# A hybrid attention and mLSTM block: the list scheduler prices TensorE's change between 512- and 128-column matmuls, and the order of all instructions is drawn anew

## The chip, the cores and the metric

The kernel runs on one core of a Trainium2 chip. A core has TensorE (PE in the profile, its weight loads PEld), VectorE (DVE), ScalarE (ACT), GpSimd (POOL) and SyncE (SP), each of which works through its own queue in order; they meet through semaphores. The metric is the device time of one execution in microseconds, as a median of runs.

## What is computed

Two layers of a decoder block on 512 tokens of width 1024, in float32. Each layer normalises its input and projects it to twelve pieces, runs two branches and adds them up behind gates:

```python
h = rmsnorm(x, norm_g)
proj = h @ w_in
aq, ak, av, az, bqk, bv, bi, bf, bo, bz, ga, gb = jnp.split(proj, idx, axis=-1)
...
oa = diff_attention(q, k, v, lam)                   # q, k: RMS-normed and rotated heads of aq, ak
oa = rmsnorm(oa, attn_norm_g) * (1.0 - lam_init)
ya = (oa * jax.nn.silu(az)) @ w_out_a
...
hb = mlstm_chunkwise(mq, mk, mv, i_pre, f_pre)      # from silu(conv(bqk)), bv, bi, bf
hb = jax.nn.sigmoid(bo) * rmsnorm(hb, mlstm_norm_g) * jax.nn.silu(bz)
yb = hb @ w_out_b
u = jax.nn.sigmoid(ga) * ya + jax.nn.sigmoid(gb) * yb
return x + u @ w_o
```

`diff_attention` takes softmax over 512 causal keys for two maps of each of eight heads, subtracts the second times `lam`, and multiplies with the values. `mlstm_chunkwise` has eight heads too; the kernel computes it as one masked 512x512 product.

## The kernel before

Precision comes from splitting: a float32 operand is stored as a high part (`wh`, `hh`, `uh`, `sdh`), cut by ScalarE, and a low part (`wl`, `hl`, `ul`, `sdl`), the difference, made by VectorE, and each product is three matmuls (high·high, low·high, high·low; `mm3`). So every block of weights of 128x1024 that SyncE fetches (`wr`) costs ScalarE one CAST of 1024 columns and VectorE one subtraction of 1024 before TensorE can use it.

Most matmuls stream 512 columns into an accumulator of one PSUM bank (pool `ps_acc`, four buffers; the names are those of the projections: qk, av, az, bqk, bv, bo, bz, ga, gb, woa, wob, wo). Between them stand the branches:

- attention, for head h and query block j: `sc` (scores, 128·(j+1) columns; one PSUM buffer), then mask, maximum, exponential and normalisation on VectorE and ScalarE into `p`, then `ut` (TensorE transposes `p` in 128x128 blocks; one PSUM buffer shared with all transposes and norm sums), split into `uh` and `ul`, then `av` (512, 384, 256 and 128 columns), then `msp_a` (a matmul with ones that sums squares across partitions) and the gated output `oa`
- mLSTM, for head h: `dd` (decay, fetched from DRAM rows and exponentiated), `ms` and `ms2` (scores of 512, 384, 256 and 128 columns), `sdh` and `sdl` (their split), `num` (512 to 128 columns), `fo_d` and `den` (the row sum, a matmul of 512 columns with ones), then `msp_b` and `ob`
- transposes of 128 columns: `ht` (the normalised input), `qkt` (rotated q and k, `rot`), `ut`, and in each layer four of `gft`, `glf` and `gct` for the gates.

A sum of squares can be folded (`fold`, `ms_front`): ScalarE squares both halves of the partitions, VectorE adds them, and high and low part share one tile of 128 partitions, so that one matmul of 512 columns does what otherwise takes two (`hi_lo`). `TUNE["foldA"]` and `TUNE["foldM"]` name the heads that fold.

The program records all operations with their dependences (`Recorder.add`), and `Recorder.schedule` then draws the order of every engine at once. It is a list scheduler with a model of time: it takes the engine that can begin first and, among the instructions of that engine whose operands the model calls ready (`rt`), the one with the lowest key. An instruction's key is its due time, propagated back from its consumers with latencies and margins, plus `TUNE["bias"]` for its kind of tile. On top come penalties that depend on the moment: `drain` if ScalarE or VectorE changes its partition offsets, `late` if the operand has been ready for less than `risk` nanoseconds, `wdiff` if the instruction isn't ready yet. An operand that another engine makes for TensorE counts as ready `pemargin` nanoseconds after it is done and the modelled latency is over. The matmul's cost in the model is its columns over 2.4 plus 13.4 ns, at least 107.5. `TUNE["order"]`, `attn`, `ml` and the other numbers set in which order the pieces of the projections are recorded and between which of them the branches' steps fall.

All recorded instructions carry line 441 in the profile (449 with the change), the line of the recorder that issues them, so tiles tell them apart and lines don't. The four-product `seven` scheme at the end (`wo`) is the same on both sides.

Of the kernel before, what the change touches and what calls it, by code (L numbers as in the profile page):

```python
# [18 lines left out]
P = 128  # L19
# [16 lines left out]

TUNE = {
    "order": (
# [4 lines left out]
    ),  # L43
    "qkt": 5,
    "gct": 15,
    "gls": 6,
    "glf": 5,
    "attn": (1, 5, 5, 8, 9, 13, 15, 16, 19, 24),
    "a0": 23,
    "ap": 18,  # L50
    "a4": 7,
    "ml": (1, 9, 11, 12, 13, 28),
    "ahead": 3,
    "lc": 7,
    "slack": 4956.0,
    "margin": 72.0,
    "pemargin": 206.2,
    "wait": 333.1,
    "swpen": 141896579.9,
    "smargin": 51.6,  # L60
    "pwait": 0.7,
    "wdiff": 3673.3,
    "wsp": 4,
    "kact": (0, 2),
    "qsq": (1, 3),
    "foldA": (2, 3, 5),
    "foldM": (0, 1, 2, 3, 4, 7),
    "foldD": (0, 1, 2, 3, 4, 5, 6, 7),
    "warm": 18,
    "start": 'x0 ct ng w0 x1 w1 x2 x3',  # L70
    "prods": 'P1 P5 P2 P6 P3 P7 P4',
    "acl": 14,
    "gateA": 9,
    "gateM": 4,
    "actp": (0, 2, 3),
    "m0": 217,
    "mp": 15,
    "m4": 9,
    "slots": 20,
    "bias": {'av': 30400.0, 'msp_a': -4350.0, 'wl': 2200.0, 'wo': -3700.0, 'woh': -4650.0, 'ht': 29250.0, 'taz': -4050.0, 'ga': 25150.0, 'gt': -8800.0, 'p': -900.0, 'wo1_P': 27550.0, 'out_0_dram': -5850.0, 'p5_wo': -4950.0, 'rot': 12400.0, 'dq': -4400.0, 'oa': 450.0, 'dd': 31000.0, 'num': 20100.0, 'ld': -7300.0, 'ws1_wo': -2200.0, 'gw': -1100.0, 'hl': -600.0, 'sc': -1500.0, 'uz': -3750.0, 'mk': 7950.0, 'sbz': 4200.0, 'az': 12900.0, 'posi': 3200.0, 'msl_d': 1650.0, 's1_wo': 5000.0, 'msh_d': 6450.0, 'sq': -1400.0, 'warm': 3150.0, 'bo': -450.0, 'sdl': 150.0, 'ml': 16100.0, 'fo_b': 12850.0, 'ws0_wo': -900.0, 'wt1_wo': 1400.0, 'pb': 8800.0, 'sbo': 5350.0, 'qkt': 3900.0, 'junk': 7400.0, 'ulZ': 6400.0, 'bv': 650.0, 'bqk': -1750.0, 'uh': -3950.0, 'ms_b': -1100.0, 'ob': -400.0, 'uy': 1500.0, 'ms': 11100.0, 'ms_a': 1750.0, 'ones': 4150.0, 'msh_b': 8300.0, 'x1d': -3000.0, 'saz': 1000.0, 'xr': -3950.0, 'wo0_P': 450.0, 'qk1_0x': 2050.0, 'msh_a': 6050.0, 'rnh': -3150.0, 'gft': 6600.0, 'gct': 3100.0, 'kl': -700.0, 'qk1_2x': -800.0, 'gf': 1550.0, 'qk0_0x': -1600.0, 'qy': 7250.0, 'msl_a': 1400.0, 'x': -4550.0, 'eps': -600.0, 'wt0_wo': -2500.0, 'xn': 400.0, 'msl_b': 2150.0, 'rn': -400.0, 'glf': -3500.0, 'ss': 7600.0, 'sinv': 6150.0, 'ulA': -2650.0, 'epsc': -3000.0, 'ulB': 950.0, 'ulY': -300.0, 'tbz': 350.0, 'hh': 3700.0, 'fo_a': 6500.0, 'mx': -1800.0, 'gc': -150.0, 'mq': -1050.0, 'ang': 3150.0, 'qt': -2500.0, 'uhZ': -1250.0, 'em': -6800.0, 'ct': 1000.0, 'fo_d': 3850.0, 'par': -250.0, 'ks': 250.0, 'den': -400.0, 'sdh': -1000.0, 'cv': -300.0, 'ng': 3750.0, 'uhB': 300.0, 'rows': -300.0, 'zw': 50.0, 'qs': 1350.0, 'ctab': 950.0, 'gcol': 3400.0, 'ul': 1000.0, 'fb_b': 400.0, 'sums': 400.0, 'cosv': 250.0},  # L80
    "drain": 467.1,
    "risk": 268.4,
    "late": 912.7,
}


# [16 lines left out]
class Recorder:  # L103
# [61 lines left out]
    def add(self, eng, e, fn, a, k):  # L165
        i = len(self.ops)
        outs = [a[0]] + ([k["accum_out"]] if k.get("accum_out") is not None else [])
        ins = [x for x in list(a[1:]) + [v for n, v in k.items() if n != "accum_out"] if isinstance(x, bass.AP)]
        if fn == "matmul" and not k["start"] or k.get("accum_op") is not None:
            ins.append(a[0])  # L170
        preds = {}
        for kind, aps in (("r", ins), ("w", outs)):
            for ap in aps:
                name, quad, mask = self.region(ap)
                ws, rs = self.acc.setdefault(name, ([], []))
                if kind == "r" and ap.space == PSUM:

                    for j, q, m in rs:
                        if self.ops[j]["eng"] != eng:
                            preds.setdefault(j, 0)  # L180
                if kind == "w":
                    for j, q, m in rs:
                        if q & quad and m & mask and j != i:
                            preds.setdefault(j, 0)
                    rs[:] = [x for x in rs if x[0] != i and (x[1] & ~quad or x[2] & ~mask)]
                for j, q, m in ws:

                    whole = kind == "r" and ap.space == PSUM and any((m >> b) & 0xFFFF and (mask >> b) & 0xFFFF for b in (0, 16))
                    if (whole or q & quad and m & mask) and j != i:
                        preds[j] = 1  # L190
                if kind == "w":
                    ws[:] = [x for x in ws if x[0] != i and (x[1] & ~quad or x[2] & ~mask)]
                    ws.append((i, quad, mask))
                else:
                    rs.append((i, quad, mask))
                t = self.tiles.get(name)
                if t is not None and (not t["ops"] or t["ops"][-1] != i):
                    t["ops"].append(i)
        if eng == "PE":

            name, _, mask = self.region(a[0])
            for b in range(2):
                if mask >> (16 * b) & 0xFFFF:
                    j = self.bank.get((name, b))
                    if j is not None:
                        preds.setdefault(j, 0)
                    self.bank[name, b] = i
        cost = self.cost(eng, fn, a, k)
        if eng == "PE":
            self.pe_time += cost  # L210
        rows = None
        if eng in ("ACT", "DVE"):

            rows = tuple(x.offset // math.prod(list(x.tensor.shape)[1:]) for x in [a[0]] + ins[:1])
        self.ops.append({"eng": eng, "e": e, "fn": fn, "a": a, "k": k, "pre": preds, "cost": cost, "nom": self.pe_time, "rows": rows, "kind": a[0].tensor.name.rstrip("_0123456789")})

    @staticmethod
    def cost(eng, fn, a, k):
# [53 lines left out]
    def schedule(self):  # L272
        ops = self.ops
# [31 lines left out]
        for i in reversed(range(n)):  # L305
            o = ops[i]
# [12 lines left out]
        table = 6  # L319
        order = []  # L320
        at_rows = {"ACT": (0, 0), "DVE": (0, 0)}

        def admit(i):

# [13 lines left out]
        while len(order) < n:  # L338
# [5 lines left out]
            for e in engs:  # L344
                c = cand[e]
                if c is None:
                    c = []
# [9 lines left out]
            s, e = best  # L357
            pick = None
            for q, i in cand[e]:
                if q <= s + (TUNE["wait"] if e != "PE" else TUNE["pwait"]):  # L360
                    k = key[i] if e != "SP" else i
                    if e in at_rows and ops[i]["rows"] != at_rows[e]:
                        k += TUNE["drain"]
                    if s - q < TUNE["risk"] and e != "SP":
                        k += TUNE["late"]
                    if e == "ACT":
                        sets = self.ACT_SET.get(self.func(ops[i]))
                        if sets and table not in sets:
                            k += TUNE["swpen"]
                    if q > s:  # L370
                        k += TUNE["wdiff"]
                    if pick is None or k < pick[0]:
                        pick = (k, i, q)
            i = pick[1]
# [4 lines left out]
            o = ops[i]  # L379
            c = o["cost"]  # L380
            if e in at_rows:
                if o["rows"] != at_rows[e]:
                    s = max(s, free[e] + 115.0)
                at_rows[e] = o["rows"]
            if e == "ACT":
                sets = self.ACT_SET.get(self.func(o))
                if sets and table not in sets:
                    s = max(s, free[e] + 1283.0)
                    table = sets[0]
                    load = table  # L390
# [1255 lines left out]
```

## Time and profile before

| | |
|---|---|
| median of 3 runs | 1333.95 us (1333.81 to 1335.08) |
| span of the profiled execution, first to last instruction | 1333.4 us |
| TensorE busy | 1326.1 us, 6200 matmuls |
| VectorE busy | 1018.1 us |
| ScalarE busy | 907.4 us, 66 table loads |
| DMA | 148.15 MB, 111 GB/s on average |

The profile has no time of its own for the profiled execution besides its span, so 0.55 us of the median lie around a span. A row of the timeline gives the start of an instruction in us from the start of the span, its duration, engine, line, operation, output and inputs (buffer numbers left out), and in square brackets how long the engine had been idle and what ended that. Matmuls overlap each other: one of 512 columns is shown with some 0.39 us while the next begins 0.23 us after it. What a matmul costs is therefore read from starts, not from durations.

### The profile page before, as it was taken

What the parts mean: (1) busy time and instruction counts of PE and PEld (TensorE: products, weight loads), DVE (VectorE), ACT (ScalarE), POOL (GpSimd) and SP (SyncE); (2) the same over time, 40 slices, a digit from 0 to 9 for tenths busy, and PEclk for the clock granted to TensorE, in tenths of its full rate; (3) what the DMA queues carried; (4) which work ended last, traced back from release to release, by engine and by line L of the source; (5) the groups of instructions that cost most, each with busy time, mean ns of one, the idle gap of its engine ahead of it and who ended that gap; (6) DMA issues with size and microseconds to landing.
All of it is one profiled execution on the core that took longest, in us unless ns stands there. A gap on an engine that the chain in (4) does not pass through costs nothing.

```text
span 1333.4 us, 17564 instructions
## 1 busy us (share of the span) xinstructions
PE 1326.1 (99%) x6200; PEld 1096.4 (82%) x6200; DVE 1018.1 (76%) x1846; ACT 907.4 (68%) x1836; POOL 37.0 (3%) x44
## 2 busy tenths in 40 slices
PE   8999999999999999999999999999999999999998
PEld 7888888888888888888888888888888888888887
DVE  7898899786259967755888988997852698687466
ACT  5878888877237958743667787888762478687243
POOL 1000000000000000000200000000000000000000
PEclk9999999999999999999999999999999999999999
DMA  5222222323344433544832121223232444345546
GB/s 188 87 65 79 80 80 64 95 79 94 100 121 124 119 114 109 154 148 123 258 125 88 49 96 54 89 67 92 82 110 81 123 134 124 98 129 148 170 123 181
DMA packets 51274, 148.15 MB, mean 111 GB/s; under 512 B 6097, under 2 KB 12881, under 8 KB 51185
## 3 DMA queue, kind: packets, MB, share of 16 engines
q1 hardware_dynamic: 48880, 138.63, 33.5%
q0 software_dynamic: 2304, 8.39, 3.5%
q8 instruction: 49, 0.80, 0.3%
q14 instruction: 41, 0.33, 0.1%
HBM read 142.74 MB, written 4.26 MB: 110 GB/s over the span
## 4 chain that ended last, share of the span: by engine, by line
PE 97%; ACT 1%; DVE 1%; DMA 0%; issue 0%; SPq 0%; DVEq 0%
PE qk L441 13%; PE av L441 9%; PE az L441 7%; PE bv L441 7%; PE bo L441 7%; PE bqk L441 7%; PE ga L441 7%; PE woa L441 7%; PE wob L441 7%; PE gb L441 6%; PE bz L441 6%; PE wo_P L441 6%; PE sc L441 3%; PE num L441 2%; PE ut L441 1%; PE ms L441 1%
## 5 line engine op out<-in xcount | busy, mean ns | idle before, releaser
L441 ACT CAST wh<-wr 128x1024 fp32r<-128x1024 f32 (+1 forms) x206 | 214.6, 1044 | 181.9 <-PE wob L441 41.0
L441 DVE TENSOR_TENSOR wl<-wr,wh 128x1024 fp32r<-128x1024 f32 (+1 forms) x208 | 249.0, 1200 | 107.1 <-ACT wh L441 106.3
L441 PE MATMUL qk<-wh,hh 128*128 128x512 f32 x256 | 96.8, 403 | 1.0 <-ACT hh L441 1.0
L441 PE MATMUL qk<-wl,hh 128*128 128x512 f32 x256 | 94.9, 397 | 0.5 <-DVE wl L441 0.5
L441 PE MATMUL qk<-wh,hl 128*128 128x512 f32 x256 | 94.9, 401 | 0.1
L441 ACT ACTIVATE p<-sc,mx,rq 128x128 f32<-128x128 f32 (+3 forms) x128 | 78.9, 619 | 18.5 <-DVE mx L441 17.8
L441 PE MATMUL woa<-oa,wh 128*128 128x512 f32 x256 | 86.4, 389 | 0.0
L441 PE MATMUL wob<-ob,wh 128*128 128x512 f32 x256 | 84.4, 389 | 0.0
L440 ACT ACT_TABLE_LOAD x65 | 83.4, 1283 | 1.1
L441 PEld LDWEIGHTS qk<-wh,hh 128*128 128x128 f32 x256 | 47.8, 189 | 11.1 <-ACT hh L441 1.3
L441 PEld LDWEIGHTS qk<-wl,hh 128*128 128x128 f32 x256 | 48.3, 189 | 9.9 <-DVE wl L441 0.9
L441 PEld LDWEIGHTS wob<-ob,wh 128*128 128x128 f32 x256 | 48.1, 188 | 10.1
L441 PEld LDWEIGHTS qk<-wh,hl 128*128 128x128 f32 x256 | 48.0, 189 | 9.9 <-DVE hl L441 0.4
L441 PEld LDWEIGHTS woa<-oa,wh 128*128 128x128 f32 x256 | 47.9, 188 | 9.9
L441 DVE TENSOR_REDUCE mx<-sc 128x2 f32<-128x256 f32 (+1 forms) x64 | 52.5, 820 | 1.1
L441 PE MATMUL bo<-hh,wl 128*128 128x512 f32 x128 | 50.3, 393 | 0.0
L441 PE MATMUL bo<-hh,wh 128*128 128x512 f32 x128 | 50.2, 392 | 0.0
L441 PE MATMUL bo<-hl,wh 128*128 128x512 f32 x128 | 50.2, 392 | 0.0
L441 PE MATMUL bqk<-hh,wl 128*128 128x512 f32 x128 | 50.0, 393 | 0.0
L441 PE MATMUL bz<-hh,wl 128*128 128x512 f32 x128 | 49.9, 393 | 0.0
L441 PE MATMUL bz<-hl,wh 128*128 128x512 f32 x128 | 49.9, 393 | 0.0
L441 PE MATMUL bz<-hh,wh 128*128 128x512 f32 x128 | 49.9, 392 | 0.0
(309 smaller groups left out, 3692.9 us busy)
## 6 DMA issues: line engine op xcount, KB each, us to landing
wr<-in_wp_dram SPq DMA_DIRECT2D x204, 512.0 KB, 3.6
ws_wo<-in_wp_dram POOLq DMA_DIRECT2D x12, 512.0 KB, 6.7
dd<-rows SPq DMA_DIRECT2D x16, 256.0 KB, 4.0
em<-rows SPq DMA_DIRECT2D x16, 256.0 KB, 3.9
dd<-rows SPq DMA_DIRECT2D x16, 192.0 KB, 5.0
x<-in_x_dram SPq DMA_DIRECT2D x4, 512.0 KB, 7.9
dd<-rows SPq DMA_DIRECT2D x16, 128.0 KB, 6.1
ws_wo<-in_wp_dram SPq DMA_DIRECT2D x4, 512.0 KB, 5.2
```

The lines of the kernel that those rows point to most:

```text
L440: self.tc.keep_in_program_order(self.nc.scalar.preload_act_table_set(self.SET_NAME[o["load"]]))
L441: self.tc.keep_in_program_order(getattr(o["e"], o["fn"])(*o["a"], **o["k"]))
```

## The change

The recorder marks a matmul as small when it streams 128 columns or fewer. While the scheduler orders TensorE, an instruction whose mark differs from that of the one before it gets `TUNE["group"]` (676.6) added to its key, so that a run of small ones, or of large ones, goes on unless another is more urgent by that much; and the model's clock is charged 22 ns at each entry from large to small. All other numbers in `TUNE` that steer the order are new as well; `drain`, `risk`, `late` and `pemargin` are lower or zero, and the two fold lists name one more head each.

```diff
@@ TUNE
-    "pemargin": 206.2,
+    "pemargin": 0.0,
-    "foldA": (2, 3, 5),
-    "foldM": (0, 1, 2, 3, 4, 7),
+    "foldA": (1, 2, 5, 6),
+    "foldM": (0, 2, 3, 4, 5, 6, 7),
-    "drain": 467.1,
-    "risk": 268.4,
-    "late": 912.7,
+    "drain": 18.4,
+    "group": 676.6,
+    "risk": 298.0,
+    "late": 592.7,
...
@@ Recorder.add
-        self.ops.append({"eng": eng, "e": e, ...
+        small = eng == "PE" and math.prod(list(a[2].shape)[1:] if fn == "matmul" else list(a[0].shape)[1:]) <= P
+        self.ops.append({"eng": eng, "small": small, "e": e, ...
...
@@ Recorder.schedule
         at_rows = {"ACT": (0, 0), "DVE": (0, 0)}
+        small = False
...
                         k += TUNE["drain"]
+                    if e == "PE" and ops[i]["small"] != small:
+                        k += TUNE["group"]
...
                 at_rows[e] = o["rows"]
+            if e == "PE":
+                if o["small"] and not small:
+                    c += 22.0
+                small = o["small"]
```

The bias table and the string of pieces, too long to show, are new throughout. The order moves on every engine; three places follow, of the order as each program is built. Numbers behind a name are the layer, the head and a buffer.

**TensorE, layer 0, around `den` of mLSTM head 6.** `num` is that head's product with the values, `ms` the next head's scores, `gb` a projection, `den` the row sum that waits for VectorE's `fo_d`. Before:

```order
L441 MATMUL num0_6_987<-sdh0_6_961,bv0_1_3_900 128x128
L441 MATMUL ms0_7_1002<-mq0_3_944,mk0_3_606 128x128
L441 MATMUL ms0_7_1002<-mql10_1_812,mk0_3_606 128x512
L441 MATMUL num0_6_987<-sdl0_6_962,bv0_1_3_900 128x128
L441 MATMUL gb0_3_981<-hl0_115,wh81_967 128x512
L441 MATMUL ms0_7_1002<-mql10_1_812,mk0_3_606 128x128
L441 MATMUL num0_6_987<-sdh0_6_961,bv0_1_3_900 128x128
L441 MATMUL num0_6_987<-sdl0_6_962,bv0_1_0_897 128x512
L441 MATMUL gb0_3_981<-hh0_114,wl81_968 128x512
L441 MATMUL gb0_3_981<-hh0_114,wh81_967 128x512
L441 MATMUL den0_6_988<-fo_d0_6_990,ones_99 128x512
```

There are three entries into 128 columns here. With the change, the `num` block of the same head, on the same engine:

```order
L449 MATMUL num0_6_992<-sdh0_6_961,bv0_1_2_890 128x256
L449 MATMUL num0_6_992<-sdh0_6_961,bv0_1_3_892 128x128
L449 MATMUL num0_6_992<-sdl0_6_962,bv0_1_3_892 128x128
L449 MATMUL num0_6_992<-sdh0_6_961,bv0_1_3_892 128x128
L449 MATMUL gb0_3_981<-hh0_114,wh81_967 128x512
```

and, 28 rows after the last of these three, the place of its row sum:

```order
L449 MATMUL gb0_2_986<-hh0_114,wl82_974 128x512
L449 MATMUL gb0_3_981<-hh0_114,wl81_968 128x512
L449 MATMUL gb0_2_986<-hh0_114,wh82_973 128x512
L449 MATMUL gb0_3_981<-hh0_114,wh81_967 128x512
L449 MATMUL den0_6_993<-fo_d0_6_995,ones_99 128x512
L449 MATMUL gb0_2_986<-hl0_115,wh82_973 128x512
```

The three small ones of `num` now follow each other, the two small ones of `ms` stand together further up, and `den` is 17 rows behind the last row of `num` where it was three.

**TensorE, layer 0, between the last transposes and the value product of attention head 7.** `ut` are the transposes, whose result ScalarE casts to `uh`, and `av` the product with it. Before:

```order
L441 MATMUL ut0_7_3_671<-ct_94,p0_7_3_655 128x128 x4
L441 MATMUL bqk0_1_670<-hh0_114,wl43_645 128x512
L441 MATMUL bqk0_1_670<-hh0_114,wh43_644 128x512
L441 MATMUL bqk0_1_670<-hl0_115,wh43_644 128x512
L441 MATMUL bqk0_1_670<-hh0_114,wl43_645 128x512
L441 MATMUL bqk0_1_670<-hh0_114,wh43_644 128x512
L441 MATMUL av0_7_676<-uh0_7_638,av0_1_0_364 128x512 x2
```

and with the change:

```order
L449 MATMUL ut0_7_3_671<-ct_94,p0_7_3_655 128x128 x4
L449 MATMUL bv0_0_3_613<-wl41_620,hh0_114 128x512
L449 MATMUL bv0_0_1_611<-wh41_619,hl0_115 128x512
L449 MATMUL bv0_0_2_612<-wh41_619,hl0_115 128x512
L449 MATMUL bv0_0_3_613<-wh41_619,hl0_115 128x512
L449 MATMUL av0_7_672<-uh0_7_638,av0_1_0_364 128x512 x2
```

Four matmuls of 512 columns cover ScalarE's cast where five did.

**ScalarE, at the start.** `wh0` is the high part of the first weights, `hh0` that of the normalised input in two halves (from the transposes `ht`), `junk0_1` and `ss0` the statistics of the second 128 tokens. Before:

```order
L441 CAST wh0_112<-wr0_110 128x1024
L441 CAST hh0_114<-ht0_0_0_118 128x4x128
L441 CAST hh0_114<-ht0_0_1_119 128x4x128
L441 ACTIVATE junk0_1_120,ss0_116<-x0_93 128x1024
L441 ACTIVATE ss0_116<-ss0_116,epsc_100 128x1
L441 ACTIVATE ss0_116<-ss0_116 128x1
L441 CAST wh1_130<-wr1_111 128x1024
```

and with the change:

```order
L449 CAST wh0_112<-wr0_110 128x1024
L449 CAST hh0_114<-ht0_0_0_118 128x4x128
L449 ACTIVATE junk0_1_120,ss0_116<-x0_93 128x1024
L449 ACTIVATE ss0_116<-ss0_116,epsc_100 128x1
L449 ACTIVATE ss0_116<-ss0_116 128x1
L449 CAST hh0_114<-ht0_0_1_119 128x4x128
L449 CAST wh1_130<-wr1_111 128x1024
```

The second half of the input's high part goes behind the statistics of the next 128 tokens; the work up to `wh1` is the same.

More of the change, by code (lines that the diff above doesn't have):

```diff
@@ L38 @@
     "order": (
[4 rows of a table removed]
[3 rows of a table added]
     ),
     "qkt": 5,
[L45 to L48, printed above, removed]
+    "gct": 20,
+    "gls": 7,
+    "glf": 9,
+    "attn": (1, 5, 5, 8, 9, 13, 16, 16, 19, 24),
     "a0": 23,
     "ap": 18,
-    "a4": 7,
-    "ml": (1, 9, 11, 12, 13, 28),
+    "a4": 9,
+    "ml": (0, 10, 10, 14, 15, 30),
     "ahead": 3,
-    "lc": 7,
-    "slack": 4956.0,
-    "margin": 72.0,
-    "pemargin": 206.2,
-    "wait": 333.1,
+    "lc": 8,
+    "slack": 5903.7,
+    "margin": 87.5,
+    "pemargin": 0.0,
+    "wait": 329.2,
     "swpen": 141896579.9,
-    "smargin": 51.6,
-    "pwait": 0.7,
-    "wdiff": 3673.3,
+    "smargin": 51.7,
+    "pwait": 0.0,
+    "wdiff": 3857.0,
     "wsp": 4,
@@ L71 @@
     "prods": 'P1 P5 P2 P6 P3 P7 P4',
-    "acl": 14,
-    "gateA": 9,
-    "gateM": 4,
+    "acl": 12,
+    "gateA": 8,
+    "gateM": 1,
     "actp": (0, 2, 3),
-    "m0": 217,
+    "m0": 220,
     "mp": 15,
-    "m4": 9,
+    "m4": 10,
     "slots": 20,
-    "bias": {'av': 30400.0, 'msp_a': -4350.0, 'wl': 2200.0, 'wo': -3700.0, 'woh': -4650.0, 'ht': 29250.0, 'taz': -4050.0, 'ga': 25150.0, 'gt': -8800.0, 'p': -900.0, 'wo1_P': 27550.0, 'out_0_dram': -5850.0, 'p5_wo': -4950.0, 'rot': 12400.0, 'dq': -4400.0, 'oa': 450.0, 'dd': 31000.0, 'num': 20100.0, 'ld': -7300.0, 'ws1_wo': -2200.0, 'gw': -1100.0, 'hl': -600.0, 'sc': -1500.0, 'uz': -3750.0, 'mk': 7950.0, 'sbz': 4200.0, 'az': 12900.0, 'posi': 3200.0, 'msl_d': 1650.0, 's1_wo': 5000.0, 'msh_d': 6450.0, 'sq': -1400.0, 'warm': 3150.0, 'bo': -450.0, 'sdl': 150.0, 'ml': 16100.0, 'fo_b': 12850.0, 'ws0_wo': -900.0, 'wt1_wo': 1400.0, 'pb': 8800.0, 'sbo': 5350.0, 'qkt': 3900.0, 'junk': 7400.0, 'ulZ': 6400.0, 'bv': 650.0, 'bqk': -1750.0, 'uh': -3950.0, 'ms_b': -1100.0, 'ob': -400.0, 'uy': 1500.0, 'ms': 11100.0, 'ms_a': 1750.0, 'ones': 4150.0, 'msh_b': 8300.0, 'x1d': -3000.0, 'saz': 1000.0, 'xr': -3950.0, 'wo0_P': 450.0, 'qk1_0x': 2050.0, 'msh_a': 6050.0, 'rnh': -3150.0, 'gft': 6600.0, 'gct': 3100.0, 'kl': -700.0, 'qk1_2x': -800.0, 'gf': 1550.0, 'qk0_0x': -1600.0, 'qy': 7250.0, 'msl_a': 1400.0, 'x': -4550.0, 'eps': -600.0, 'wt0_wo': -2500.0, 'xn': 400.0, 'msl_b': 2150.0, 'rn': -400.0, 'glf': -3500.0, 'ss': 7600.0, 'sinv': 6150.0, 'ulA': -2650.0, 'epsc': -3000.0, 'ulB': 950.0, 'ulY': -300.0, 'tbz': 350.0, 'hh': 3700.0, 'fo_a': 6500.0, 'mx': -1800.0, 'gc': -150.0, 'mq': -1050.0, 'ang': 3150.0, 'qt': -2500.0, 'uhZ': -1250.0, 'em': -6800.0, 'ct': 1000.0, 'fo_d': 3850.0, 'par': -250.0, 'ks': 250.0, 'den': -400.0, 'sdh': -1000.0, 'cv': -300.0, 'ng': 3750.0, 'uhB': 300.0, 'rows': -300.0, 'zw': 50.0, 'qs': 1350.0, 'ctab': 950.0, 'gcol': 3400.0, 'ul': 1000.0, 'fb_b': 400.0, 'sums': 400.0, 'cosv': 250.0},
@@ L81 @@
-    "drain": 467.1,
-    "risk": 268.4,
-    "late": 912.7,
+    "bias": {'av': 33680.0, 'wl': 7000.0, 'wo': -3700.0, 'woh': -4650.0, 'taz': -5720.0, 'oa': -2580.0, 'msl_d': 1650.0, 'msh_d': 6450.0, 'uh': -7560.0, 'kl': 11110.0, 'lq': -37100.0, 'qk': 57430.0, 'wh': -1020.0, 'rnh': -5640.0, 'wob': 910.0, 'uz': -9830.0, 'junk': 9520.0, 'hl': 92930.0, 'qk1_0x': 4830.0, 'em': 1880.0, 'bv': 16860.0, 'p5_wo': -7450.0, 'mql': 61640.0, 'ht': 20290.0, 'fo_b': -6350.0, 'rot': 18970.0, 'out_0_dram': -4390.0, 'sq': 1940.0, 'fb_d': 39020.0, 'num': 53580.0, 'msh_a': -6400.0, 'msp_b': 82520.0, 'uhZ': 30080.0, 'saz': 17550.0, 'rn': 12690.0, 'rows': -15020.0, 'ones': -73230.0, 'ulY': -1230.0, 'xn': 9900.0, 'msl_a': 33250.0, 'gt': -7940.0, 'ms': -9720.0, 'sbo': -11640.0, 'p': 25480.0, 'stab': -11620.0, 'gb': 12870.0, 'x1d': 4210.0, 'mq': 20030.0, 'ulB': 80170.0, 'sgb': -13540.0, 'qkt': 23990.0, 'den': -15330.0, 'qss': 550.0, 'gm': -1080.0, 'pb': -10650.0, 'dd': -3010.0, 'posf': -58570.0, 'wo0_P': -4810.0, 'par': 8350.0, 'sdl': -30170.0, 'gft': 16770.0, 'ws0_wo': 26650.0, 'hh': 1340.0, 'sdh': 18320.0, 'mk': 8340.0, 'glf': -5110.0, 'woa': -570.0, 'qy': -1170.0, 'zw': -4320.0, 'ng': -3580.0, 'gi': 29810.0, 'gct': 12090.0, 'gc': 5030.0, 'ms_b': 14620.0, 'ld': 51060.0, 'gf': 13440.0, 'az': -2970.0, 'tbz': -2290.0, 'rq': 42630.0, 'gcol': 29700.0, 'ml': 57060.0, 'qk0_0x': -910.0, 'ga': -370.0, 'gw': 10220.0, 'uhA': 18570.0, 'ct': 170.0, 'wo1_P': 35850.0, 'qs': -7480.0, 'cv': -4130.0, 'warm': -4750.0, 'uhB': 11790.0, 'bz': -14250.0, 'zeroc': 14570.0, 'posi': -2300.0, 'sinv': -4580.0, 'eps': 25330.0, 'qk1_2x': -3080.0, 'fo_a': -160.0, 'wr': 9940.0, 'fo_d': 9330.0, 'sums': 11640.0, 'ob': -7850.0, 'ang': 4270.0, 'uhY': -9300.0, 'xr': -7730.0, 'sbz': -13840.0, 'ks': -5890.0, 'ws1_wo': -11010.0, 'epsc': 8130.0, 'msp_a': -1390.0, 'ulZ': 19300.0, 'ctab': -2560.0, 'msl_b': 300.0, 'wt1_wo': 12820.0, 'fb_a': 660.0, 'ss': 12980.0, 'wt0_wo': 600.0, 'ul': -850.0, 'ut': 18300.0, 'bo': -2890.0, 'ulA': 12540.0, 'ua': -1710.0, 'bqk': 3040.0, 'qt': 2960.0, 'sc': 6490.0, 'uy': 2210.0, 'fb_b': 8740.0, 'dq': -3650.0, 'msh_b': -860.0, 'qk0_2x': 0.0, 'cosv': 990.0, 's1_wo': 8660.0, 'lneps': -1810.0, 'x': 800.0},
@@ L214, in add @@
             rows = tuple(x.offset // math.prod(list(x.tensor.shape)[1:]) for x in [a[0]] + ins[:1])
-        self.ops.append({"eng": eng, "e": e, "fn": fn, "a": a, "k": k, "pre": preds, "cost": cost, "nom": self.pe_time, "rows": rows, "kind": a[0].tensor.name.rstrip("_0123456789")})
+        small = eng == "PE" and math.prod(list(a[2].shape)[1:] if fn == "matmul" else list(a[0].shape)[1:]) <= P
+        self.ops.append({"eng": eng, "small": small, "e": e, "fn": fn, "a": a, "k": k, "pre": preds, "cost": cost, "nom": self.pe_time, "rows": rows, "kind": a[0].tensor.name.rstrip("_0123456789")})
     @staticmethod
```

7 rows, old and new, of the table TUNE are left out of this document.

## The prediction

> **What bounds the kernel.** I read the page first: the shares, the clock and the chain that ended last.
>
> ```profile
> span 1333.4 us, 17564 instructions
> PE 1326.1 (99%) x6200; PEld 1096.4 (82%) x6200; DVE 1018.1 (76%) x1846; ACT 907.4 (68%) x1836; POOL 37.0 (3%) x44
> ...
> PEclk9999999999999999999999999999999999999999
> ...
> PE 97%; ACT 1%; DVE 1%; DMA 0%; issue 0%; SPq 0%; DVEq 0%
> ```
>
> TensorE is busy 99% of the span and is 97% of the last chain, at full clock. So the time is TensorE's own work plus the moments in which it waits, and VectorE (76%) and ScalarE (68%) matter only where they make it wait. The list of TensorE's waits has very little:
>
> ```profile
> PE qk L441 <- ACT hh L441: 1.0, 1, 1.0
> PE qk L441 <- DVE wl L441: 0.5, 1, 0.5
> PE ht L441 <- DVE junk L441: 0.3, 1, 0.3
> ```
>
> All three are in the first 13 us; the fourth row, 1.6 us before the first warm-up matmul, stays. This view hides short waits, because matmuls overlap in the rows: a wait under 0.16 us (0.39 shown, 0.23 from start to start) leaves no gap. I therefore went through the starts on the timeline. What a matmul costs, from a run of large ones (five steps between the first two rows), and from single and fourfold small ones between large ones:
>
> ```profile
> 461.79 0.39 PE L441 MATMUL bz<-hh,wl 128*128 128x512 f32 x1
> ...
> 462.92 0.39 PE L441 MATMUL bz<-hl,wh 128*128 128x512 f32 x1
> 463.28 0.70 PE L441 MATMUL num<-sdh,bv 128*128 128x512 f32 x2
> ```
>
> ```profile
> 952.36 0.39 PE L441 MATMUL bv<-wl,hh 128*128 128x512 f32 x1
> 952.60 0.27 PE L441 MATMUL ut<-ct,p 128*128 128x128 f32 x1
> 952.62 0.47 PE L441 MATMUL bv<-wh,hl 128*128 128x512 f32 x1
> 952.94 0.39 PE L441 MATMUL bv<-wh,hh 128*128 128x512 f32 x1
> 953.17 0.27 PE L441 MATMUL ut<-ct,p 128*128 128x128 f32 x1
> 953.20 0.47 PE L441 MATMUL bv<-wh,hh 128*128 128x512 f32 x1
> 953.51 0.63 PE L441 MATMUL bv<-wl,hh 128*128 128x512 f32 x2
> ```
>
> ```profile
> 912.97 0.39 PE L441 MATMUL az<-hl,wh 128*128 128x512 f32 x1
> 913.20 0.60 PE L441 MATMUL ut<-ct,p 128*128 128x128 f32 x4
> 913.56 0.48 PE L441 MATMUL ga<-hh,wl 128*128 128x512 f32 x1
> 913.87 0.40 PE L441 MATMUL az<-hh,wl 128*128 128x512 f32 x1
> ```
>
> A large one costs (462.92 − 461.79)/5 = 0.226 us. The `ut` at 952.60 looks almost free, since the next begins 0.02 us later, but the large one behind it then takes 0.32: the small one's price shows one step late. So I count from a large one to the second large one behind. From 952.36 to 953.51 stand four large and two small: 1.15 − 4 × 0.226 = 0.246, or 0.123 for a single one. From 912.97 to 913.87 stand two large and four small: 0.90 − 0.452 = 0.448. Three more small ones thus cost 0.325, which is 0.108 each, and a single one 0.015 more than that. This 0.015 is the price of an entry into 128 columns.
>
> **Entries.** In TensorE's order, runs of matmuls of 128 columns or fewer number 254 before and 191 with the change; singles fall from 121 to 34, the number of small matmuls stays 568. That removes 63 entries. The two passages taken apart (952.36 to 952.94, then to 953.51) give 0.020 and 0.010, so the bounds are 0.6 and 1.3 us. I take 0.012, near the lower end, since a large step is 0.226 in the long run but reads 0.23 in many rows, which eats into the difference: 63 × 0.012 = **−0.8 us**.
>
> [...]
>
> **Folding.** The square sums go through these groups:
>
> ```profile
> L441 PE MATMUL msp_b<-fo_b,ones 128*128 128x512 f32 x12 | 4.8, 397 | 0.0
> L441 PE MATMUL msp_a<-msh_a,ones 128*128 128x512 f32 x10 | 4.0, 404 | 0.0
> ...
> L441 PE MATMUL msp_a<-fo_a,ones 128*128 128x512 f32 x6 | 2.5, 422 | 0.0
> L441 PE MATMUL msp_b<-msh_b,ones 128*128 128x512 f32 x4 | 1.6, 397 | 0.0
> ```
>
> One more head folds in each branch and layer, so four of the high parts' 14 matmuls, and with them their low parts, become four folded ones: eight go, four come. Four large matmuls fewer are 4 × 0.226 = **−0.9 us**. VectorE and ScalarE each get four instructions more, on engines that are idle 24% and 32%; without that cover, the chain behind one head would be some 0.6 us longer.
>
> **The wait at `den`.** The longest wait behind the start is that of head 6's row sum, in both layers:
>
> ```profile
> 545.34 0.69 DVE L441 TENSOR_TENSOR fo_d<-dd,fo_d 64x512 fp32r<-64x512 f32 x1
> 545.56 0.40 PE L441 MATMUL gb<-hh,wh 128*128 128x512 f32 x1
> 546.08 0.50 PE L441 MATMUL den<-fo_d,ones 128*128 128x512 f32 x1
> 546.42 0.40 PE L441 MATMUL gb<-hh,wh 128*128 128x512 f32 x1
> ```
>
> ```profile
> 1204.21 0.69 DVE L441 TENSOR_TENSOR fo_d<-dd,fo_d 64x512 fp32r<-64x512 f32 x1
> 1204.50 0.40 PE L441 MATMUL gb<-hh,wh 128*128 128x512 f32 x1
> 1204.95 0.50 PE L441 MATMUL den<-fo_d,ones 128*128 128x512 f32 x1
> 1205.29 0.39 PE L441 MATMUL gb<-hh,wh 128*128 128x512 f32 x1
> ```
>
> From `gb` to the `gb` behind `den` pass 0.86 and 0.79 us where two steps need 0.45: 0.41 + 0.34, about 0.75 us in all. In the new order `den` stands 17 rows behind `num` and not three, and between the end of `ms2`, which starts its chain, and `den` lie matmuls of some 2.5 us more. But VectorE too has four instructions more there (24, not 20), and its mean is 1018.1/1846 = 0.55 us, so 2.2 us more. The two nearly cancel. I take **0** with both ends open: −0.75 if the wait goes, +0.9 if those four are of the longest kind and it doubles.
>
> **Thinner cover.** The scheduler used to treat an operand for TensorE as ready 206 ns later than modelled; that is now zero, and the `late` penalty is a third lower. At attention head 7 the cast and the product that needs it read:
>
> ```profile
> 306.13 0.48 ACT L441 CAST uh<-ut 128x384 fp32r<-128x384 f32 x1
> ...
> 307.08 0.40 PE L441 MATMUL av<-uh,av 128*128 128x512 f32 x1
> ```
>
> The cast ends at 306.61, 0.47 before TensorE uses it, with five matmuls between transposes and product. With four, 0.47 − 0.23 = 0.24 is left. How close can it get? At `den`, `fo_d` ended at 1204.90 and TensorE went on at 1204.95, so an operand is in use 0.05 after it is done. A guard of 0.24 still holds if ScalarE is as punctual as here; where an engine runs more than 0.19 late, TensorE now waits. Nothing in the trace of before shows how often that is; the bounds are 0 and, as a far end, a wait of 0.2 us at a quarter of the chains. There are in two layers 64 from scores to `ut`, 32 to `qkt`, and 16 each to `av`, `msp_a`, `den` and `msp_b`, together 160, so 40 × 0.2 = 8 us. The nearest row is this one, which says no wait; I take **+0.5**, about one wait of `den`'s size more.
>
> **The start.** ScalarE casts the second half of `hh0` three instructions later, and the statistics of the next tokens earlier. That half is first needed by the third block of weights, so the move is harmless, and the statistics would let the 0.3 us at `ht` go. VectorE's second half of `wl0` moves ahead of one other subtraction, which takes from the 0.5 us at `wl`. Against it stands the clock:
>
> ```profile
> 5.28:8.69 3.41, 3.13 (x19) 2.35 (x17) 1.41 (x2) 1.02 (x5) 0.00 (x0) 1.00 1.01 366
> 8.69:12.10 3.41, 1.90 (x7) 0.78 (x5) 2.49 (x4) 3.35 (x8) 0.00 (x0) 1.00 1.02 416
> 12.10:15.52 3.42, 3.40 (x12) 2.81 (x13) 3.32 (x7) 2.81 (x7) 0.00 (x0) 0.50 0.69 203
> ```
>
> (The columns: stretch, its length, busy time of TensorE, weight loads, VectorE, ScalarE and GpSimd with counts, granted clock, DMA share, GB/s.) A stretch with TensorE busy 1.90 of 3.41 us is followed by one at half clock. There the matmuls are stretched, but they wait for data anyway, since DMA is saturated (1.02) until 12.1 and ScalarE is full (3.35 of 3.41). All 18 warm-up matmuls now stand ahead of the transposes, where two used to stand between and behind them, so the idle gap ahead of 10 us grows. I take **0**: −0.8 if both waits go, +1.7 if a second stretch falls to half clock (half of 3.42).
>
> [...]
>
> **Sum.** −0.8 − 0.9 + 0 + 0.5 + 0 = −1.2 us against the profiled execution: a span of 1332.2. With the 0.55 us that the median has beyond the span, the forecast is **1332.7 us**, against 1333.95 now. A measurement of this kernel can tell about 0.2% from no change, which is 2.67 us, so this is no change: 1331.28 to 1336.62.
>
> **Rivals.**
>
> - Everything old goes and nothing new comes: −0.8 − 0.9 − 0.75 at `den` − 0.8 at the start = −3.25, **1330.7 us**. For it speaks that the small groups became as tidy as meant and that `den` has more room; against it that VectorE's share of that room grew too, and that so many waits would have to go at once. Chance 0.30.
> - TensorE runs into its operands: the guard that was given up is needed. In the attention chains VectorE and ScalarE deliver `p`, `uh` and `fo_a` with 0.24 us to spare and are often later. At 0.2 us each, 22 waits among the 160 turn the −1.7 of the first two terms into more than +2.67; 32 give 6.4 and **1338.6 us**. For it: the zero in `pemargin`, and `av` one matmul nearer. Against it: the room from scores to transposes did not shrink in general. Chance 0.22.
> - The change doesn't do what it says: an entry costs nothing of its own, and the 0.015 is rounding. Then −0.9 + 0.5: **1333.5 us**, inside no change. Chance 0.10. [...]
> - A second stretch at half clock: −1.2 + 1.7, **1334.4 us**, no change too. Chance 0.08.
>
> My forecast has the rest, 0.30. So faster 0.30, same 0.30 + 0.10 + 0.08 = 0.48, slower 0.22. The range must leave out no more than 0.2: below, all terms at their good ends give 1333.95 − 1.3 − 0.9 − 0.75 − 0.8 = 1330.2, and I go to 1329.8; above, it takes in most of the second rival, to 1338.0.
>
> **What would show it.** Entry term: single `ut` rows nearly gone, and the price of a large-small-large passage unchanged at 0.12 for one and 0.45 for four. Folding: 24 rows of `msp_a` and 18 of `msp_b` where 26 and 20 stood. `den`: steps of 0.23 around it in head 6. Guard: the steps ahead of `ut`, `av`, `msp_a` and `qkt`; if they exceed 0.23 at more than 20 places, the second rival holds. Start: the first `qk` matmul again near 10.1 us, and one stretch at half clock. The forecast is wrong if TensorE's waits behind 20 us change by more than 1.5 us in sum either way.

## The result, and the profile after

The changed kernel takes **1344.26 us** (median of 5 runs, 1342.89 to 1345.57) against 1333.95: ratio 1.0077, 95% interval 1.0064 to 1.0089. It is slower by 10.3 us, where 1332.7 was forecast and 1338.0 was the top of the range. The page of its profiled execution, in the lines that were shown of before:

```profile
span 1343.8 us, 17571 instructions
PE 1330.9 (99%) x6196; PEld 1091.3 (81%) x6196; DVE 1022.6 (76%) x1850; ACT 909.8 (68%) x1840; POOL 36.9 (3%) x44
...
PE 84%; DMA 6%; DVE 4%; ACT 3%; SPq 1%; issue 1%; DVEq 0%; ACTq 0%
```

The shares of busy time say nothing, as before. The chain that ended last says it: TensorE has 84% of it instead of 97%, and DMA, VectorE and ScalarE now stand in it with 13%. TensorE's list of waits (total, times, longest) has new rows:

```profile
PE ms L449 <- DVE dd L449: 3.5, 6, 0.8
PE qk L449 <- ACT hh L449: 1.7, 1, 1.7
...
PE num L449 <- DVE ms_b L449: 1.6, 2, 0.9
PE den L449 <- DVE fo_d L449: 0.6, 2, 0.3
PE bz L449 <- ACT wh L449: 0.2, 1, 0.2
```

The `qk` row is the start. The others are all in the mLSTM heads. How much of the loss is there shows in busy time by stretches, for the stretch of the mLSTM heads in each layer (columns: stretch, length, busy time and count of TensorE, weight loads, VectorE, ScalarE, GpSimd, then granted clock, DMA share, GB/s). Before:

```profile
390.00:575.00 185.00, 184.88 (x857) 153.75 (x856) 151.26 (x213) 140.38 (x198) 3.77 (x4) 1.00 0.44 125
...
1055.00:1240.00 185.00, 184.94 (x857) 153.76 (x856) 148.48 (x209) 139.33 (x196) 3.63 (x4) 1.00 0.45 127
```

After:

```profile
390.00:575.00 185.00, 181.82 (x833) 148.44 (x833) 143.04 (x202) 133.62 (x188) 1.87 (x2) 1.00 0.40 115
...
1055.00:1240.00 185.00, 182.27 (x835) 148.77 (x834) 143.57 (x202) 134.68 (x189) 1.72 (x2) 1.00 0.42 118
```

In the same 185 us TensorE begins 24 and 22 matmuls fewer. At 185/857 = 0.216 us each that is 5.2 + 4.7 = 9.9 of the 10.4 us between the two spans, or some 9 when the narrower ones among them are counted at less. Everything outside these stretches nearly balances.

What VectorE waits for in them is one row in each list, before and after:

```profile
DVE dd L441 <- DMA dd<-rows: 1.5, 2, 0.8
```

```profile
DVE dd L449 <- DMA dd<-rows: 11.8, 11, 1.8
```

`dd` is the decay tile of a head. SyncE fetches four pieces of it from `rows`, and VectorE adds the mask (`dd<-dd,ct`) in step `decay`. Head 5 of layer 0 on the timeline after:

```profile
490.03 1.78 SPq L449 DMA_DIRECT2D dd<-rows  x4
```

```profile
498.22 0.42 DVE L449 TENSOR_TENSOR dd<-dd,ct 128x256 f32<-128x256 f32 x1 [1.76 <-DMA dd<-rows]
...
498.68 0.40 ACT L449 ACTIVATE dd<-dd,gcol 128x128 f32<-128x128 f32 x1 [0.95 <-DVE dd L449]
...
500.05 1.23 DVE L449 TENSOR_TENSOR wl<-wr,wh 128x1024 fp32r<-128x1024 f32 x1 [1.41 <-ACT wh L449]
...
501.20 1.22 DVE L449 SCALAR_TENSOR_TENSOR dd<-ms,dd 128x1024 f32<-128x1024 f32 x1
501.32 0.39 PE L449 MATMUL num<-sdh,bv 128*128 128x512 f32 x1
...
502.47 0.39 PE L449 MATMUL ms<-mq,mk 128*128 128x256 f32 x1 [0.76 <-DVE dd L449]
```

Read it downwards. The mask add stands in VectorE's queue before its data are there and holds the queue for 1.76 us. ScalarE's exponential and its cast `wh` come late by that, then VectorE's `wl`, then the product of scores and decay at 501.20, which empties the PSUM tile that the next `ms` needs. From `num` at 501.32 to `ms` at 502.47 pass 1.15 us where 0.23 is a step. Ten such stalls, of 0.47 to 1.07 us over the step, stand in the two layers, 7.3 us in all, each 3 to 5 us behind one of the waits for `dd<-rows`.

The scheduler believed otherwise. In its model a transfer from `rows` takes its bytes at 175 bytes per ns, one behind the other, and lands 2000 ns later: 655,360 bytes make 3.7 + 2.0 = 5.7 us from the first of the four issues. The wait above ended 498.22 − 490.03 = 8.2 us behind it; of the other ten, nine ended between 8.0 and 9.0 us behind the first issue, and one, for the first pieces of a tile, after 7.0. So an order that looks free of waits in the model has them on the chip, if it puts the add soon behind the fetch. Before stood near that edge as well, but behind it only twice:

```profile
489.14 1.85 SPq L441 DMA_DIRECT2D dd<-rows  x4
...
533.17 1.85 SPq L441 DMA_DIRECT2D dd<-rows  x4
```

```profile
498.60 0.42 DVE L441 TENSOR_TENSOR dd<-dd,ct 128x256 f32<-128x256 f32 x1
...
541.90 0.43 DVE L441 TENSOR_TENSOR dd<-dd,ct 128x256 f32<-128x256 f32 x1 [0.77 <-DMA dd<-rows]
```

The first add comes 9.5 us behind its fetch and doesn't wait; the second, 8.7 behind, does. The transfers themselves are hardly slower than before: the four pieces land 4.0, 5.0, 6.1 and 7.1 us after their own issues before (medians), and 4.0, 5.2, 6.3 and 7.1 after. What has changed is the distance between fetch and add.

### The profile page after: what moved, and what is told of

Its sections match the earlier page's. It is cut to its first block, busy times and chain, and to the rows that moved or that the text cites. A ratio compares the mean times of both kernels' runs of the same rounds, so it can differ in the third digit from the quotient of the medians.

```text
span 1343.8 us, 17571 instructions
## 1 busy us (share of the span) xinstructions
PE 1330.9 (99%) x6196; PEld 1091.3 (81%) x6196; DVE 1022.6 (76%) x1850; ACT 909.8 (68%) x1840; POOL 36.9 (3%) x44
## 4 chain that ended last, share of the span: by engine, by line
PE 84%; DMA 6%; DVE 4%; ACT 3%; SPq 1%; issue 1%; DVEq 0%; ACTq 0%
PE qk L449 13%; PE av L449 9%; PE az L449 7%; PE ga L449 7%; PE gb L449 7%; PE wob L449 6%; PE bv L449 6%; PE wo_P L449 6%; DMA dd<-rows 5%; PE bqk L449 5%; PE woa L449 4%; PE bo L449 3%; PE sc L449 3%; PE bz L449 3%; PE num L449 2%; PE ut L449 1%
## 5 line engine op out<-in xcount | busy, mean ns | idle before, releaser
L449 PE MATMUL woa<-oa,wh 128*128 128x512 f32 x256 | 82.4, 391 | 0.0
L449 PE MATMUL wob<-ob,wh 128*128 128x512 f32 x256 | 81.5, 389 | 0.0
L449 PEld LDWEIGHTS wob<-ob,wh 128*128 128x128 f32 x256 | 48.1, 188 | 10.3 <-DVE ob L449 0.3
L449 PE MATMUL az<-hh,wh 128*128 128x512 f32 x128 | 50.3, 401 | 0.0
L449 PE MATMUL bqk<-hh,wh 128*128 128x512 f32 x128 | 50.3, 396 | 0.0
```

The source lines that it names most:

```text
L449: self.tc.keep_in_program_order(getattr(o["e"], o["fn"])(*o["a"], **o["k"]))
```

## The experiments

Three theories. **1:** the order places the mask adds before the fetch can have landed. **2:** the guard for TensorE (`pemargin`) that was given up is needed. **3:** the rule itself moves matmuls to bad places.

**SyncE's queue alone.** In `issue`, behind the schedule (`wr` is a weight fetch, `heads` the heads of the four entries behind it):

```diff
+ sp = [(p, i) for p, i in enumerate(order) if self.ops[i]["eng"] == "SP"]
+ for q, (p, i) in enumerate(sp[:-4]):
...
+     if self.ops[i]["kind"] == "wr" and all(self.ops[j]["kind"] == "dd" for _, j in sp[q + 1 : q + 5]) and len(heads) == 1:
+         order[p], moved = None, sp[q + 4][0]
+         order[moved] = (order[moved], i)
```

> The kernel after, with one change on SyncE's queue alone: where the four fetches of a decay tile dd stand right behind a weight fetch wr, the wr goes behind the four. The rows of TensorE, VectorE and ScalarE stay as they are. Theory 1 (VectorE's mask add on dd stands in its queue before the fetch dd<-rows has landed, 11 waits of 11.8 us in the profile of after, and TensorE stalls for 7.3 us behind them): the fetches of heads 1, 3 and 5 of both layers no longer wait for a wr to come free and land earlier; the three stalls of each layer behind them (0.48, 0.75, 0.92 and 0.47, 0.64, 0.98 us, 4.2 us) go, the waits for dd<-rows fall from 11.8 to about 6 us, and the time is 1340.0 (1339 to 1342). Theory 2 (the guard for TensorE of 206 ns that is given up) and theory 3 (the grouping rule moves matmuls to bad places): no row of a computing engine moves, so 1344.3 within 1.

Measured: 1363.98 us, ratio 1.0227 (1.0209 to 1.0245), far outside every expectation. The rule moved twelve weight fetches and not six: those at heads 0, 4 and 6 of each layer went too. The waits for `dd<-rows` fell to 4.7 us, and the stalls behind heads 1, 3 and 5 were gone. But at heads 0 and 6 the fetch was waiting for its own tile to come free, and now the weights stood behind it. Two rows of TensorE's waits (one wait in each layer), and ScalarE's cast at head 0:

```profile
PE msp_a L456 <- ACT msh_a L456: 9.8, 2, 5.0
PE num L456 <- DVE ms_b L456: 8.5, 2, 4.4
```

```profile
309.40 1.05 ACT L456 CAST wh<-wr 128x1024 fp32r<-128x1024 f32 x1 [4.77 <-DMA wr<-in_wp_dram]
```

So the fetches that were pulled forward in SyncE's queue held what stood behind them until their own tile was free: ScalarE stood for 4.77 us ahead of the cast. The test was spoiled by its side effect, so it was narrowed.

**Heads 1, 3 and 5 alone.** The same lines with one more condition (`heads` now holds the head's number):

```diff
- and len(heads) == 1:
+ and len(heads) == 1 and heads.pop() in "135":
```

> The kernel after, with SyncE's queue changed as in the first experiment, but for heads 1, 3 and 5 alone, where the profile of after shows the fetch waiting only for its turn behind a wr and not for its own tile. In the first experiment the waits of TensorE behind these heads were gone, and the 5 us stalls it brought stood at heads 0 and 6. Theory 1: stalls of 4.2 us go and nothing new comes but a wr that is 1.9 us later: 1340.0 (1338.5 to 1342.0), waits for dd<-rows 4 to 7 us. Theories 2 and 3: no row of a computing engine moves, 1344.3 within 1.

Measured: **1339.06 us**, ratio 1.0035 (1.0022 to 1.0047). That is 5.2 us less than after, with six weight fetches moved and the order of TensorE, VectorE and ScalarE the same row for row. The place of head 5 again:

```profile
497.33 1.22 DVE L456 SCALAR_TENSOR_TENSOR dd<-ms,dd 128x1024 f32<-128x1024 f32 x1
...
498.55 0.39 PE L456 MATMUL num<-sdh,bv 128*128 128x512 f32 x1
498.78 0.28 PE L456 MATMUL ms<-mq,mk 128*128 128x256 f32 x1
```

From `num` to `ms` it is one step of 0.23 instead of 1.15, since `dd<-ms,dd` now begins 1.22 us ahead of `num` and not 0.12. Waits for `dd<-rows` are down to 3.7 us, at heads 6 and 7, with 2.5 us of TensorE still behind them. Theory 1 holds for these stalls; theories 2 and 3 allowed no change here. Since the two orders of TensorE are the same, the profiles can be laid side by side, matmul by matmul. Of the 6.8 us between their spans (1343.8 and 1337.0), 4.3 arise at the six stalls and 1.0 in the first 15.3 us, where this execution had no stretch at half clock (granted clock 1.0 in the mean). That 1.0 isn't due to the change.

**The landing in the model.**

```diff
- end[i] = max(dma, go) + 2000.0
+ end[i] = max(dma, go) + 2000.0 + (3000.0 if str(o["kind"]) == "dd" else 0.0)
```

> The kernel after, with the scheduler's landing time of the fetch dd<-rows set 3000 ns later (5000 instead of 2000 behind the transfer), nothing else. Every engine's order follows from it. Theory 1: the mask adds move down VectorE's queue to where the fetch has landed, the waits for dd<-rows fall from 11.8 to under 2 us, TensorE's waits for ms, num and den go with them (7.3 us), and the time is 1337 (1335 to 1339). Theories 2 and 3: guard and rule are as in after, so TensorE's stalls stay somewhere: 1342 to 1346.

Measured: 1341.96 us, ratio 1.0058 (1.0041 to 1.0076). The mechanism was as theory 1 said: the lists show no wait for `dd<-rows` any more, nor one for `ms`, `num` or `den`. The time was not, because the last head now feeds the output product late:

```profile
PE wob L449 <- ACT ob L449: 2.9, 2, 1.4
PE wob L449 <- DVE ob L449: 1.7, 2, 0.8
```

From start to start these are 1.59 + 1.12 us over the step in each layer, 5.4 in all. So waits came back at the end of the chain, and only 2.3 us were gained.

**The rule alone.** Against before, with the lines of the scheduler that the change adds:

```diff
+ "group": 676.6,
...
+     if e == "PE" and ops[i]["small"] != small:
+         k += TUNE["group"]
...
+     if o["small"] and not small:
+         c += 22.0
```

> The numbers of before with the new rule alone (676.6 per switch and 22 ns per entry); TensorE enters matmuls of 128 columns 220 times instead of 254. Theory 1 and theory 2: nothing that feeds the mask adds has changed (dd keeps its 31000, the guard its 206), so 34 entries fewer at 0.012 us, 0.4 us: 1333.5 (1332 to 1335). Theory 3: most of the 10.3 us comes with the rule: 1339 or more.

Measured: 1335.47 us, ratio 1.0011 (1.0001 to 1.0021): 1.4 us more than the kernel before beside it, just above what theories 1 and 2 gave, and far from theory 3. TensorE's list has 1.5 us more at `ht` than before and 1.0 less at `qk`, all in the first 14 us, and this execution isn't behind there: by 20 us it has begun 70 matmuls, that of before 66. New behind the start are two waits at `msp_a`, one in each layer, 0.53 and 0.68 us over the step.

**The rule taken out of the kernel after.**

```diff
- "group": 676.6,
+ "group": 0.0,
...
-     c += 22.0
+     c += 0.0
```

> The numbers of after with the rule taken out (0 per switch, 0 ns per entry); 262 entries instead of 191. Theory 1: the mask adds stand as early as before, so the waits for dd<-rows stay at 8 to 14 us; 71 entries more are 0.9 us: 1345 (1342 to 1348). Theory 2: the same, from the guard: 1345. Theory 3: 1336 or less.

Measured: 1362.45 us, ratio 1.0211 (1.0194 to 1.0229), a miss for all three. The waits for `dd<-rows` stayed (11.3 us), which theory 1 had; but stalls came that none had foreseen, the longest at `ga`, which waits for `wl` (two, 2.7 us each over the step). So the rule isn't what costs: with the other new numbers it saves 18 us. Without it the same numbers draw another order, with stalls of its own.

**The guard back.**

```diff
- "pemargin": 0.0,
+ "pemargin": 206.2,
```

> The kernel after, with the guard of 206.2 ns back (the scheduler takes what other engines make as ready for TensorE 206 ns later), nothing else; 194 entries. Theory 1: the mask adds do not wait for TensorE's guard, the waits for dd<-rows stay at 8 to 14 us, and the time is 1344 or more (1343 to 1352). Theory 2 (the guard given up is what costs): 1338 or less.

Measured: 1354.84 us, ratio 1.0152 (1.0137 to 1.0167). The guard makes it 10.6 us worse, more than theory 1's range, and the fetch is waited for as before:

```profile
DVE dd L449 <- DMA dd<-rows: 12.3, 8, 2.2
```

TensorE's list also has the two `wob` rows of the later landing again (2.9 and 1.7 us) and longer waits for `ms` and `num`. So giving the guard back doesn't help, and theory 2 falls as it was put. What the guard is worth by itself this run can't say, since the whole order is drawn anew with it.

**Numbers fitted anew.** Two kernels whose scheduler knows a later landing, with `bias` and the small numbers beside it chosen again in the scheduler's own model of time, from the numbers of after and of before. Some of their lines, with the numbers rounded, for after and then for before:

```diff
- end[i] = max(dma, go) + 2000.0
+ end[i] = max(dma, go) + 2000.0 + (2727.2 if str(o["kind"]) == "dd" else 0.0)
- "pemargin": 0.0,
+ "pemargin": 27.9,
- "group": 676.6,
+ "group": 709.8,
...
```

```diff
- end[i] = max(dma, go) + 2000.0
+ end[i] = max(dma, go) + 2000.0 + (3958.2 if str(o["kind"]) == "dd" else 0.0)
- "pemargin": 206.2,
+ "pemargin": 210.8,
+ "group": 475.1,
...
```

> The kernel after (its piece order, folds, steps and rule) with the landing of dd<-rows set 2727 ns later in the scheduler, and the bias list and the small numbers beside it (slack, margins, guard 27.9, drain, risk, late) fitted anew to a scheduler that knows this landing; 200 entries. Theory 1: waits for dd<-rows under 2 us, TensorE's waits for ms, num and den gone, no new tail before wob: 1333 (1331 to 1336), level with before. Theory 2 (thin guard, 28 ns here) : stalls of other kinds stay, 1339 or more. Theory 3 (the rule, 710 per switch here): 1339 or more.

> The piece order, folds and steps of before, with the rule at 475 per switch (no charge per entry), the landing of dd<-rows 3958 ns later in the scheduler, and the bias list and the small numbers fitted anew as in the run beside it; 205 entries instead of 254. Theory 1: the two waits of before for dd<-rows (1.5 us, with 0.5 us of TensorE behind them) go, 49 entries fewer at 0.012 us are 0.6 us, and the small stalls thin out: 1332.8 (1331.5 to 1334.0). Theory 3: 1339 or more, since the rule is in.

Measured: from after 1337.6 us, ratio 1.0029 (1.0017 to 1.0041), 1.6 us above the top that theory 1 gave; from before 1334.02, ratio 1.0001 (0.9992 to 1.0010), no difference, at the top of what theory 1 gave. The rule is in both, and neither comes to the 1339 that theory 3 asked for. In the second too no wait for `dd<-rows` and none at `den` is left, and that brought no gain that can be measured. In the first, the waits for `dd<-rows` and the stalls in the heads are gone, and one new stall stands near the end, behind another fetch:

```profile
1306.38 1.05 ACT L449 CAST wh<-ws_wo 128x1024 fp32r<-128x1024 f32 x1 [1.93 <-DMA ws_wo<-in_wp_dram]
...
1309.35 0.50 PE L449 MATMUL wo_P<-wh,ulB 128*128 128x512 f32 x1 [1.89 <-DVE xr L449]
```

So after's piece order and folds can be had within 4 us of before, once the landing is right and the other numbers are fitted to it. No version that was run beats before by more than the measurement can tell.

## Why the prediction was wrong, step by step

**Thinner cover: the step that failed.** The prediction asked how far ahead of TensorE its direct operands are made, looked at the attention chains (`p`, `uh`, `fo_a`), and put +0.5 us on it. What came was 7.3 us, in the mLSTM heads, from a transfer two engines upstream. So the sign that the prediction named for a wrong forecast was met: the listed waits of TensorE behind 20 us went from none to 5.9 us. Its sign for the rival with the guard, long steps ahead of `ut`, `av`, `msp_a` and `qkt` at more than 20 places, was not. Of the passages from one large matmul to the next that take over 40 ns more than their steps, six end at `msp_a`, where two did before, and none at the value product `av`, where two did; the steps from large matmuls into `ut` and `qkt` are too long by that much at three places, as at three before. That rival had the sign of the result and a time of 1338.6, but not its mechanism: the stalls aren't in the attention chains, and the kernel with the guard back takes another 10.6 us. (One of the scheduler's numbers, `risk`, rose, from 268.4 to 298.0, where the section on the change counts it among those that are lower.) Forecast and rivals all lacked the question what VectorE and ScalarE wait for.

**`den`.** Half right: head 6's wait is gone in both layers, as hoped, and a new one of 0.48 and 0.47 us over the step stands at head 0. But the row that would have led to the cause was next to the rows quoted. In before, the add at 541.90 that waits 0.77 us for its fetch is that of head 7, and it stands in VectorE's queue ahead of head 6's `fo_d` at 545.34. From there to `fo_d` VectorE has next to no pause. The wait at `den` was put down to how much VectorE has to do (24 instructions or 20), when by these rows a fetch had made it late.

**Entries.** Right in size and too small to be seen. From the first matmul's start to the last's, less every passage that is over 40 ns longer than its steps (0.226 for a large one, 0.108 for a small one), there remain:

| kernel | entries | large matmuls of 512 | remains, us |
|---|---|---|---|
| before | 254 | 5248 | 1317.05 |
| the rule alone | 220 | 5248 | 1316.63 |
| after without the rule | 262 | 5244 | 1317.52 |
| after | 191 | 5244 | 1316.92 |
| after, heads 1, 3 and 5 moved | 191 | 5244 | 1316.74 |

The rule alone gives 0.42/34 = 0.012 an entry, the figure that was taken; the last two rows against the one without the rule give 0.60/71 = 0.008 and 0.78/71 = 0.011. The differences in the last column are good to some 0.1 us, by what step the matmuls of 256 and 384 columns are counted at, so this bears out a hundredth of a microsecond and no finer figure.

**Folding.** Done as described: 24 rows of `msp_a` and 18 of `msp_b`. Its 0.9 us don't show. With entries and folding, 1317.05 − 0.8 − 0.9 = 1315.4 should remain, and after has 1316.92, 1.5 us more, spread over steps that are each less than 40 ns long. Where these come from stays open.

**The start.** As forecast, about 0: in both profiles one stretch ran at half clock (0.53 here from 12.10 to 15.52, 0.50 before). The longer wait for `hh`, 1.7 instead of 1.0 us, is made up for by the 0.5 at `wl` and the 0.3 at `ht` that went. That the two profiles agree here is in part luck: with the same order at the start, heads 1, 3 and 5 moved, no stretch ran at half clock, and TensorE was 1.0 us further on at 15.3 us. So the order alone doesn't settle it, and what does isn't shown.

**The offset.** The prediction took 0.55 us around the span. In all runs here, of before too, it is 1.72 to 1.83: the profiled execution of before, with its span of 1333.4, was the longest of its three. The forecast doesn't depend on it, since either way it comes to the median of before less the 1.2 us of the sum.

**The account.** Of 10.5 us between first and last matmul, the ten stalls behind the fetch make 7.3, less the 0.5 at head 6's `den` that went. Passages of 0.04 to 0.13 us too much grew from 30 to 57 behind the first 20 us, from 2.4 to 5.1 us. The rest is small and of both signs. Of the ten stalls, six are shown to hang on the fetch by moving fetches alone. The four at heads 6 and 7 are put down to it by their rows; in the order with the later landing they are gone, but that order is another one throughout. Why the short passages became more isn't shown. Which of the numbers moves the adds forward isn't settled: with `dd` of the bias list at 31000 again the scheduler draws the same order, row for row, so it isn't that one alone.

## What to carry to other kernels

When an order is drawn by a model, compare the model's figures with the trace before pricing the moves: a landing that is 2 to 3 us too early in the model (5.7 us there, mostly 8.0 to 9.0 in the traces) did little harm while the order happened to leave slack there, and cost TensorE a stall at ten of the sixteen heads when another order left less. Follow each engine that feeds the bound one back to its own waits; a row of 0.77 us on an engine that isn't the bottleneck showed here the edge that the next order crossed. And a fetch moved ahead in SyncE's queue kept ScalarE waiting 4.77 us for the weights behind it at head 0 here: look first whether what it passes may wait as long as its own tile does.

## What the runs showed of the hardware that was not expected

**A queue of fetches landed late.** The four pieces of `dd` landed 4.0, 5.2, 6.3 and 7.1 us after their own issues (medians after; 256, 192, 128 and 64 KB), so the smallest took longest:

```profile
dd<-rows SPq DMA_DIRECT2D x16, 256.0 KB, 4.0
dd<-rows SPq DMA_DIRECT2D x16, 192.0 KB, 5.2
dd<-rows SPq DMA_DIRECT2D x16, 128.0 KB, 6.3
dd<-rows SPq DMA_DIRECT2D x16, 64.0 KB, 7.1
```

The scheduler's model has all four down 5.7 us behind the first issue; at head 5 of layer 0 the wait for them ended 8.2 us behind it. No run has one of these transfers alone, so what 64 KB take by themselves isn't shown.

**A long stall cost again in clock.** Where TensorE stood for some 5 us, at head 0 in the first experiment, the two stretches behind ran at half clock, 0.50 and 0.51 (0.990 in the mean of the execution):

```profile
308.00:313.20 5.20, 1.76 (x8) 1.13 (x6) 1.29 (x2) 3.77 (x5) 0.00 (x0) 0.99 0.32 119
313.20:316.60 3.40, 2.05 (x5) 1.67 (x6) 3.15 (x5) 3.33 (x6) 0.00 (x0) 0.50 0.17 18
316.60:320.00 3.40, 3.40 (x10) 2.62 (x9) 2.09 (x4) 2.38 (x5) 0.00 (x0) 0.51 0.37 136
320.00:323.40 3.40, 3.40 (x17) 2.80 (x16) 1.46 (x3) 1.74 (x4) 0.00 (x0) 1.00 0.00 0
```

In the kernel after without the rule (0.997 in the mean) one stretch did, 0.52, behind a stall of 2.7 us, and the same again in the other layer:

```profile
218.90:222.30 3.40, 0.89 (x3) 0.37 (x3) 3.08 (x6) 2.81 (x15) 0.00 (x0) 0.98 0.00 0
222.30:225.70 3.40, 3.40 (x11) 2.59 (x10) 2.42 (x9) 2.07 (x5) 0.00 (x0) 0.52 0.50 154
```

Between 316.60 and 320.00 TensorE began 10 matmuls where 17 follow at full clock, so the 3.4 us cost 7/17 of their length there, about 1.4 us. In the kernel after no stretch from 15.52 to 1343 us ran at half clock (1.00); the row below has its longest wait behind the start, 0.91 us at `num`:

```profile
519.50:522.90 3.40, 2.49 (x11) 1.79 (x10) 1.84 (x3) 2.75 (x5) 0.00 (x0) 1.00 0.54 154
```

**The same order at the start ran at two clocks.** The kernel after and the first experiment have the same order there. After:

```profile
8.69:12.10 3.41, 1.76 (x6) 0.98 (x6) 2.17 (x4) 3.35 (x7) 0.00 (x0) 0.97 1.02 414
12.10:15.52 3.42, 3.42 (x13) 2.56 (x12) 3.42 (x7) 3.39 (x8) 0.00 (x0) 0.53 0.68 194
```

The first experiment:

```profile
8.69:12.10 3.41, 2.25 (x8) 0.97 (x6) 2.67 (x5) 3.35 (x8) 0.00 (x0) 1.00 1.03 420
12.10:15.52 3.42, 3.16 (x16) 2.28 (x17) 3.42 (x7) 3.00 (x7) 0.00 (x0) 1.00 0.69 189
```

TensorE was busy for 1.76 us of the first stretch in the one and 2.25 in the other, and the second had a clock of 0.53 and of 1.00. The kernel fitted anew from before had 2.80 and 1.00. These are single executions; what sets the clock they don't show.
